# Decoder layer with sliding-window attention and retention: bursts of matmuls joined, a quad's vector work handed out in parts

## The chip, the cores and the metric

The kernel runs on one core of one Trainium2 chip. Measured is the device time of one execution in microseconds (us); smaller is better. The profile is of one execution on the same core.

## What is computed

One decoder layer on 256 tokens of width 2048: a SwiGLU feed-forward, a token-mixing part, a second feed-forward, each behind an RMS norm with scale and shift from a condition vector. The change touches the token mixing alone:

```python
rq, rk, rv, rg, sq, sk, sv, gl_ret, gl_swa = jnp.split(h @ w_in, IN_SPLITS, axis=-1)
# retention, 8 heads: q and k 128 wide (rotary), v 256 wide, two chunks of 128 tokens
ro = retention_chunkwise(rq, rk, rv)          # decayed scores @ v, no softmax
ro = ro * rsqrt(mean(ro * ro, -1) + eps)
# attention: 32 query heads, 8 key/value heads, 64 wide, window 128, one sink per head
logits = einsum('bnqhgd,bnkhd->bnhgqk', qb, kb) * d ** -0.5     # masked to the window
probs = softmax(concatenate([logits, sink], -1))[..., :-1]
out = einsum('bnhgqk,bnkhd->bnqhgd', probs, vb)
merged = sigmoid(gl_ret) * (ro' @ w_ret_branch) + sigmoid(gl_swa) * (out @ w_swa_branch)
```

All is float32 in and out.

## The kernel before

**The main work.** Every large product is a chain of weight blocks. `load` (L344 to L347) fetches a block of 512 rows by 512 columns, 1 MB, with a DMA that SyncE (SP) issues into one of four `raw` tiles. A block is used in two halves of 256 rows. For a half, `split` (L365 to L373) makes the pair `wh` and `wl`: ScalarE casts the half to the matmul's format (L369, `wh`), VectorE subtracts to get the rest (L371, `wl`). Pool `wsp` holds three such pairs. `products` (L349) then issues 12 matmuls of 512 columns for the half on TensorE: L356 and L357 read `wh`, L359 reads `wl`. `gemm_part` (L408) does one block: two halves, and a call of `tick` (L313) behind each. `gemm` calls `step` (L334) behind each block, which advances whatever generator stands first in the list `side`. So one block is one step of side work. The `raw` tiles are shared with the rows of `w_ada`, which a second stream (`conditioning`, L214 and L219) reads in the background.

**The side work.** While the blocks of `w_in` run, `softmax_heads` (L1321) does the attention: eight "quads" of four heads, four steps (parts 0 to 3) for a quad. For quad g:

- part 0, `quad_weights`: matmuls of queries and keys (L1229) into two banks of `psd` and two of `psm`; VectorE scales and masks them into `logits` (L1237), takes maxima (L1249 to L1253); ScalarE does the exponentials (L1258); VectorE adds and inverts the sums (L1262, L1263) and multiplies (L1265, two instructions).
- part 2, `quad_apart`: four ScalarE copies (L1279) split the words of the probabilities into the two planes of `planes_of`.
- part 2 of the next quad, `quad_turn`: two DMA transposes (L1288) issued by SP, from `planes_of` into tiles `a`. In that part `quad_turn` of the quad before comes ahead of `quad_apart` of this one.
- part 3 of the next quad, `quad_together`: four VectorE copies (L1300).
- part 1 two quads later, `quad_values`: matmuls of probabilities and values (L1313) and one copy (L1317).

`logits`, `planes_of` and `turned_p` exist once. After the quads come the eight heads of `retention` (L1395): step one makes the scores (L1398, L1401) and multiplies them by the decay; step two makes the values (L1411 to L1413), a root, and a scaling.

**What sets the order.** SP issues strictly in the order in which the program is written (L102). On the other engines a scheduler places instructions by priority and by its own estimate of when they are ready; `issue_after(x)` puts an instruction behind x on its engine. Every engine executes its instructions in the order in which they stand.

Of the kernel before, what the change touches and what calls it, by code (L numbers as in the profile page):

```python
# [17 lines left out]
P = 128  # L18
# [59 lines left out]
def layer_kernel(  # L78
# [57 lines left out]
    def a512():  # L136
        return t512()
# [1079 lines left out]
    halves = [slice(i * HD, (i + 1) * HD) for i in range(2)]  # L1217
    asked, dec = set(), []

    def quad_weights(g):  # L1220

        assert g // 2 in asked
        late = [side_bank() for _ in range(2)]
        early_q = [bank() for _ in range(2)]
        with tc.issue_after(newest[-1]), tc.high_priority(offset=300):
            for ps, qs, n in ((late, slice(P, S), S), (early_q, slice(0, P), P)):
                for a in range(2):
                    for i, hs in enumerate(halves):
                        nc.tensor.matmul(  # L1229
                            ps[i][:, a * n : (a + 1) * n],  # L1230
                            qo[hs, 2 * g + a, qs], skt[hs, g, :n], start=True, stop=True,
                        )
        by_half = logits.rearrange("p (a i) n -> p a i n", a=2)
        for ps, ns in ((late, slice(P, W3)), (early_q, slice(0, P))):
            n = ns.stop - ns.start
            for i in range(2):
                nc.vector.scalar_tensor_tensor(  # L1237
                    out=by_half[:, :, i, ns],
                    in0=ps[i][:, : 2 * n].rearrange("p (a n) -> p a n", a=2),
                    scalar=HD**-0.5,  # L1240
                    in1=mask[:, None, ns].broadcast_to([P, 2, n]),
                    op0=ALU.mult,
                    op1=ALU.add,
                )
        mx, ng, se, sm = (small(2 * HQ, tag) for tag in ("mx", "ng", "se", "sm"))
        m2, n2, s2 = (v.rearrange("p (t i) -> p t i", t=2) for v in (mx, ng, se))
        parts_of = (logits[:, :, :P], logits[:, :, P:])
        for t, of_t in enumerate(parts_of):
            nc.vector.tensor_reduce(out=m2[:, t, :], in_=of_t, axis=AX.X, op=ALU.max)  # L1249
        sb = sink_b[:, HQ * g : HQ * (g + 1)][:, None, :].broadcast_to([P, 2, HQ])  # L1250
        nc.vector.tensor_tensor(out=m2, in0=m2, in1=sb, op=ALU.max)
        nc.vector.tensor_scalar(out=ng, in0=mx, scalar1=-1.0, scalar2=None, op0=ALU.mult)
        nc.vector.tensor_tensor(out=s2, in0=n2, in1=sb, op=ALU.add)  # L1253
        nc.scalar.activation(se, se, AF.Exp)
        for t, of_t in enumerate(parts_of):
            for i in range(HQ):
                z = t * HQ + i
                nc.scalar.activation(  # L1258
                    of_t[:, i, :], of_t[:, i, :], AF.Exp,
                    bias=ng[:, z : z + 1], accum_out=sm[:, z : z + 1],  # L1260
                )
        nc.vector.tensor_add(sm, sm, se)  # L1262
        nc.vector.reciprocal(sm, sm)  # L1263
        for t, of_t in enumerate(parts_of):
            nc.vector.tensor_tensor(  # L1265
                out=of_t, in0=of_t,
                in1=sm[:, t * HQ : (t + 1) * HQ][:, :, None].broadcast_to(
                    [P, HQ, of_t.shape[2]]
                ),
                op=ALU.mult,  # L1270
            )

    def quad_apart():

        with tc.issue_after(cast[-1]):
            for a in range(2):
                src = logits[:, 2 * a : 2 * a + 2, :].rearrange("p h n -> p (h n)")
                for i in range(2):
                    nc.scalar.copy(planes[:, a, i, :], words(src)[:, :, i])  # L1279

    def quad_turn():

        turned = [pair_tile() for _ in range(2)]
        turned = [
            t.rearrange("p i n -> p (i n)").bitcast(U16)[:, : 4 * W3] for t in turned
        ]
        for a in range(2):
            nc.sync.dma_start_transpose(  # L1288
                turned[a].rearrange("p (k n) -> p k n", n=P),
                planes[:, a].rearrange("p i n -> p (i n)"),  # L1290
            )
        return turned

    def quad_together(turned):

        for a in range(2):
            into = turned_p[:, 2 * a : 2 * a + 2].rearrange("p h b q -> p (h b q)")
            with tc.issue_after(low[-1]):
                for i in range(2):
                    nc.vector.tensor_copy(  # L1300
                        words(into)[:, :, i], turned[a][:, i * 2 * W3 : (i + 1) * 2 * W3]
                    )

    def quad_values(g):

        po = bank()
        p4 = po.rearrange("p (a t q) -> p a t q", a=2, t=NT)
        vs = slice(g * HD, (g + 1) * HD)
        heads = turned_p.rearrange("p (a i) b q -> p a i b q", a=2)
        with tc.issue_after(newest[-1]), tc.high_priority(offset=300):  # L1310
            for t, blk, tv in ((0, 0, 0), (1, 1, 0), (1, 2, 1)):
                for i in (1, 0):
                    nc.tensor.matmul(  # L1313
                        p4[halves[i], :, t, :], sv[:, tv, vs], heads[:, :, i, blk, :],
                        start=blk < 2, stop=blk != 1,
                    )
        nc.any.tensor_copy(  # L1317
            qo[:, 2 * g : 2 * g + 2, :].rearrange("p a s -> p (a s)"), po
        )

    def softmax_heads():  # L1321

        turned = {}
        for at in range(4 * (QUADS + 1) + 2):
            g, part = divmod(at, 4)
            if part == 0 and g < QUADS:
                quad_weights(g)
            if part == 1 and g >= 2:
                quad_values(g - 2)
            if part == 2 and g >= 1:  # L1330
                turned[g - 1] = quad_turn()
            if part == 2 and g < QUADS:
                quad_apart()
            if part == 3 and g >= 1:
                quad_together(turned.pop(g - 1))
                if g == QUADS:
# [55 lines left out]

    vo = slot().rearrange("p (t n) -> p t n", t=NT)

    def retention(h):  # L1395
        assert {(0, h // 4), (1, h // 4)} <= kept
        ps = side_bank()
        nc.tensor.matmul(  # L1398
            ps[:, :S], qk[:, 1, h, :P], qk[:, 0, h, :], start=True, stop=True
        )  # L1400
        nc.tensor.matmul(  # L1401
            ps[:, S : S + P], qk[:, 1, h, P:], qk[:, 0, h, P:], start=True, stop=True
        )
        sc = a512()
        dh = dec[0][:, h * S : (h + 1) * S]
        nc.vector.tensor_mul(sc[:, :S], ps[:, :S], dh)
        nc.vector.tensor_mul(sc[:, S : S + P], ps[:, S : S + P], dh[:, :P])
        yield
        hv = slice(h * RDV, (h + 1) * RDV)
        po = side_bank()  # L1410
        nc.tensor.matmul(po[:, :RDV], sc[:, :P], vo[:, 0, hv], start=True, stop=True)  # L1411
        nc.tensor.matmul(po[:, RDV:], sc[:, P:S], vo[:, 0, hv], start=True, stop=False)  # L1412
        nc.tensor.matmul(  # L1413
            po[:, RDV:], sc[:, S : S + P], vo[:, 1, hv], start=False, stop=True
        )
        v = small(NT, "rvar")
        junk = a512()
        for t in range(NT):
            nc.scalar.activation(
                junk[:, t * RDV : (t + 1) * RDV],  # L1420
                po[:, t * RDV : (t + 1) * RDV],
                AF.Square,
                accum_out=v[:, t : t + 1],
            )
# [12 lines left out]
        yield  # L1437

    for ci in range(4):
        b = in_chunk(O_RV + ci * CH)  # L1440
        for t in range(NT):
            nc.any.tensor_copy(vo[:, t, ci * CH : (ci + 1) * CH], b[t])
        side += [retention(h) for h in (2 * ci, 2 * ci + 1)]

    def gates(p):

# [171 lines left out]
```

## Time and profile before

| | us |
|---|---|
| median of 3 runs (lowest, highest) | 2374.83 (2372.2, 2376.29) |
| the profiled execution, whole | 2372.74 |
| span of its instructions | 2370.9 |
| TensorE (PE) busy in it | 2343.8 (99%) |
| VectorE (DVE) busy | 1702.1 (72%) |
| ScalarE (ACT) busy | 1313.8 (55%) |
| first L1229 to last L1229 | 876.4 to 1052.7 |
| last L1313 | 1109.1 |

A row of a timeline holds the start, the duration, the engine, the line, the operation, the tiles written and read, a count, and in brackets how long the engine stood idle ahead of it and for whom. SPq is SyncE's queue of DMA issues, PEld the weight load of a matmul. A row of waits holds who waited for whom, the sum, how often, and the longest.

### The profile page before, as it was taken

The page shows a single profiled execution, that of the slowest core. Times are in us where ns is not written, and L with a number is a line of the kernel's source. Part 1 is how long each engine was busy: PE and PEld are TensorE (multiplying, and loading weights), DVE is VectorE, ACT ScalarE, POOL GpSimd, SP SyncE. Part 2 cuts the span into 40 slices and gives each one's busy share as a digit, 9 for nine tenths or more (in the row PEclk, how much of TensorE's full clock was granted, in tenths as well). Part 3 has the DMA queues.
Part 4 walks back from the last instruction along what each step waited for, and adds up shares of the span by engine and source line. Part 5 has one row for each costly group of instructions (what it writes and reads, how often), then busy time and mean ns, then how long its engine had stood idle before and what let it go on. Part 6 is the DMA issues. An engine that isn't in the chain of part 4 may idle for free.

```text
span 2370.9 us, 28253 instructions
## 1 busy us (share of the span) xinstructions
PE 2343.8 (99%) x10431; PEld 1917.6 (81%) x10431; DVE 1702.1 (72%) x2624; ACT 1313.8 (55%) x1782; POOL 9.2 (0%) x21
## 2 busy tenths in 40 slices
PE   8999999999999999999999999999999999999998
PEld 5888888888788887778888888888888888888886
DVE  7887799778877768976777776677555555555656
ACT  6544456455546568775556564466455455455544
POOL 0000000000000000000000000000000000000000
PEclk9999999999999999999999999999999999999999
DMA  9987789998866788877778787755677777766553
GB/s 367 366 294 264 272 292 343 356 351 336 312 248 241 274 281 235 252 223 244 270 274 294 297 299 281 289 197 185 240 240 250 253 241 247 245 220 203 192 198 124
DMA packets 186316, 627.87 MB, mean 265 GB/s; under 512 B 108801, under 2 KB 109185, under 8 KB 115649
## 3 DMA queue, kind: packets, MB, share of 16 engines
q1 hardware_dynamic: 183682, 615.05, 74.7%
q0 software_dynamic: 1600, 9.83, 1.2%
q8 instruction: 82, 1.34, 0.2%
q10 hardware_dynamic: 896, 1.19, 0.1%
q14 instruction: 56, 0.46, 0.1%
HBM read 597.16 MB, written 4.22 MB: 254 GB/s over the span
## 4 chain that ended last, share of the span: by engine, by line
PE 54%; DVE 1%; DMA 0%; issue 0%; ACT 0%; DVEq 0%; SPq 0%
PE pa L359 18%; PE pa L356 18%; PE pa L357 18%; DMA slot<-in_w_ada_dram 0%; DVE wl L371 0%; PE ps L1313 0%; PE pd L1411 0%; PE pd L1413 0%; PE pd L1412 0%; PE pd L1398 0%; PE ps L832 0%; DVE home L465 0%; ACT wh L369 0%; DVE soft L1300 0%; DVE slot L219 0%
## 5 line engine op out<-in xcount | busy, mean ns | idle before, releaser
L369 ACT CAST wh<-raw 128x1024 fp32r<-128x1024 f32 x792 | 832.0, 1053 | 913.2 <-PE pa L357 888.6
L371 DVE TENSOR_TENSOR wl<-raw,wh 128x1024 fp32r<-128x1024 f32 x792 | 961.1, 1222 | 520.3 <-ACT wh L369 518.5
L356 PE MATMUL pa<-wh,hh 128*128 128x512 f32 x2184 | 854.1, 391 | 2.4 <-ACT wh L369 2.4
L357 PE MATMUL pa<-wh,hl 128*128 128x512 f32 x2184 | 850.4, 389 | 0.0
L359 PE MATMUL pa<-wl,hh 128*128 128x512 f32 x2184 | 773.6, 391 | 2.6 <-DVE wl L371 2.4
L356 PEld LDWEIGHTS pa<-wh,hh 128*128 128x128 f32 x2184 | 410.0, 188 | 91.0 <-ACT wh L369 3.7
L359 PEld LDWEIGHTS pa<-wl,hh 128*128 128x128 f32 x2184 | 408.4, 188 | 92.8 <-DVE wl L371 7.0
L357 PEld LDWEIGHTS pa<-wh,hl 128*128 128x128 f32 x2184 | 410.1, 188 | 84.6 <-issue 0.2
L357 PE MATMUL pa<-wh,a 128*128 128x512 f32 x944 | 366.2, 389 | 0.0
L356 PE MATMUL pa<-wh,a 128*128 128x512 f32 x944 | 349.9, 390 | 1.8 <-DVE t L622 1.8
L359 PE MATMUL pa<-wl,a 128*128 128x512 f32 x944 | 348.4, 390 | 1.9 <-DVE wl L371 1.9
L219 DVE CUSTOM_DVE_ANT_0 slot<-slot,cact 128x512 f32<-128x512 f32 (+2 forms) x272 | 209.7, 819 | 22.5 <-DMA slot<-in_w_ada_dram 22.4
L359 PEld LDWEIGHTS pa<-wl,a 128*128 128x128 f32 x944 | 177.0, 188 | 39.8 <-DVE wl L371 3.4
L356 PEld LDWEIGHTS pa<-wh,a 128*128 128x128 f32 x944 | 177.0, 188 | 39.2 <-DVE t L622 2.2
L357 PEld LDWEIGHTS pa<-wh,a 128*128 128x128 f32 x944 | 177.3, 188 | 37.9 <-DVE a L405 1.3
L530 ACT COPY slot<-back 128x512 uint16<-128x512 uint16 x140 | 93.3, 766 | 0.0
L219 DVE CUSTOM_DVE_ANT_0 rows_x<-rows_x,cact 128x512 f32<-128x512 f32 x124 | 78.7, 686 | 13.3 <-DMA rows_x<-in_w_ada_dram 13.1
L219 DVE CUSTOM_DVE_ANT_0 raw<-raw,cact 128x512 f32<-128x512 f32 (+1 forms) x108 | 70.8, 706 | 16.1 <-DMA raw<-in_w_ada_dram 16.1
L405 DVE TENSOR_TENSOR a<-slot,a 128x512 fp32r<-128x512 f32 x118 | 80.5, 684 | 0.3
L514 ACT COPY flat<-t 128x512 uint16<-128x512 uint16 x128 | 72.7, 617 | 3.6 <-DVE t L1386 2.8
L404 ACT CAST a<-slot 128x512 fp32r<-128x512 f32 x118 | 72.7, 617 | 0.1
L219 DVE DVE_READ_ACCUMULATOR2_ANT sums<- 128x1 f32 x504 | 41.0, 81 | 0.0
(228 smaller groups left out, 1169.1 us busy)
## 6 DMA issues: line engine op xcount, KB each, us to landing
raw<-in_w_ffn_gu_dram SPq DMA_DIRECT2D x160, 1024.0 KB, 5.1
raw<-in_w_in_dram SPq DMA_DIRECT2D x104, 1024.0 KB, 5.7
raw<-in_w_ffn_down_dram SPq DMA_DIRECT2D x88, 1024.0 KB, 4.9
slot<-in_w_ada_dram SPq DMA_DIRECT2D x83, 1024.0 KB, 7.2
rows_x<-in_w_ada_dram SPq DMA_DIRECT2D x31, 1024.0 KB, 7.1
raw<-in_w_ada_dram SPq DMA_DIRECT2D x26, 1024.0 KB, 5.6
raw<-in_w_swa_branch_dram SPq DMA_DIRECT2D x16, 1024.0 KB, 6.8
raw<-in_w_ret_branch_dram SPq DMA_DIRECT2D x16, 1024.0 KB, 5.6
```

What stands on the lines that cost most here:

```text
L219: nc.vector.tensor_tensor_reduce(out=w[:, at], in0=w[:, at], in1=cact[:, at], scale=1.0, scalar=0.0, op0=ALU.mult, op1=ALU.add, accum_out= ...
L356: nc.tensor.matmul(ps, ah[:, j, ts], wh[:, j, :], start=first, stop=False)
L357: nc.tensor.matmul(ps, al[:, j, ts], wh[:, j, :], start=False, stop=False)
L359: nc.tensor.matmul(ps, ah[:, j, ts], wl[:, j, :], start=False, stop=last).ins
L369: cast.append(nc.scalar.copy(hi, src).ins)
L371: low.append(nc.vector.tensor_sub(lo, src, hi.bitcast(F32)).ins)
L404: nc.scalar.copy(hi, v)
L405: nc.vector.tensor_sub(lo, v, hi.bitcast(F32))
L514: nc.scalar.copy(planes[:, i, :], words(src)[:, :, i])
L530: nc.scalar.copy(into[:, :, :, i], held["turned"][:, i])
```

## The change

For the quads, the class `Quad` takes the place of `quad_weights`, `quad_apart`, `quad_turn` and `quad_together`. The matmuls of the values of quad g-2 and of the logits of quad g are issued by one call, `quad_burst`, in part 0, and share the two banks of `psm`; the values' copy is two ScalarE copies in part 2. The vector work is put into a list `trickle`, from which `tick` takes one entry behind each half of a block. The sink is negated once, which lets two VectorE instructions of a quad fall away. For retention, `head_burst` issues the values of head h-2 with the scores of head h, a step for a head, 11 steps in place of 16.

```diff
+    trickle = []
+
     def tick():
+        if trickle:
+            trickle.pop(0)()
...
+    def quad_burst(g, gv):
...
+        late = [side_bank() for _ in range(2)] if g is not None else None
+        both = [bank() for _ in range(2)]
         with tc.issue_after(newest[-1]), tc.high_priority(offset=300):
+            if gv is not None:
...
+                            both[t][halves[i], S:].rearrange("p (a q) -> p a q", a=2),
+                            sv[:, tv, vs], heads[:, :, i, blk, :],
...
+            if g is not None:
+                assert g // 2 in asked
+                for ps, qs, n in ((late, slice(P, S), S), (both, slice(0, P), P)):
...
             g, part = divmod(at, 4)
-            if part == 0 and g < QUADS:
-                quad_weights(g)
-            if part == 1 and g >= 2:
-                quad_values(g - 2)
-            if part == 2 and g >= 1:
-                turned[g - 1] = quad_turn()
-            if part == 2 and g < QUADS:
-                quad_apart()
-            if part == 3 and g >= 1:
-                quad_together(turned.pop(g - 1))
...
+            now, past = quads.get(g), quads.get(g - 1)
+            assert not trickle
+            if part == 0:
+                late, both = quad_burst(
+                    g if g < QUADS else None, g - 2 if g >= 2 else None
+                )
...
+                if past:
+                    trickle.extend([lambda: past.apart(0), lambda: past.apart(1)])
+            if part == 1:
+                if past:
+                    past.turn()
+                if now:
+                    trickle.extend([now.masked, now.greatest])
...
+            if part == 2 and g >= 2:
+                quad_out(g - 2, both)
+            if part == 2 and now:
+                trickle.extend([lambda: None, lambda: now.powers(0)])
+            if part == 3:
+                def parts(i):
+                    if now and i == 0:
+                        now.powers(1)
+                    if past:
+                        past.together(i)
+                    if now and i == 1:
+                        now.shares()
+
+                trickle.extend([lambda: parts(0), lambda: parts(1)])
```

`apart` is the four ScalarE copies (now L1329), `turn` the two transposes (now L1338), `shares` the sum, reciprocal and multiplications (now L1313 to L1316), each with the instructions that it had, but for two small VectorE ones.

SP, at the transposes of the second quad (g = 1), before. `raw` blocks count up in the order of their numbers; `a` are the tiles that the transposes of a quad write, `back` those of other transposes:

```order
L346 DMA raw_7208<-in_w_in_dram 128x2048
L346 DMA raw_7288<-in_w_in_dram 128x2048
L519 DMA_TRANSPOSE back_7322<-flat_7027 128x8x128
L346 DMA raw_7335<-in_w_in_dram 128x2048
L519 DMA_TRANSPOSE back_7370<-flat_7104 128x8x128
L1288 DMA_TRANSPOSE a_7372<-planes_of 128x12x128
L1288 DMA_TRANSPOSE a_7373<-planes_of 128x12x128
L346 DMA raw_7380<-in_w_in_dram 128x2048
```

ScalarE, before, at the copies that fill `planes_of` for these transposes:

```order
L369 CAST wh_7210<-raw_7208 128x1024
L1279 COPY planes_of<-soft 128x768 x4
L369 CAST wh_7227<-raw_7208 128x1024
L530 COPY slot_6287<-back_7102 128x4x128 x2
L530 COPY slot_6287<-back_7144 128x4x128 x2
L369 CAST wh_7290<-raw_7288 128x1024
L369 CAST wh_7306<-raw_7288 128x1024
L514 COPY flat_7247<-t_7192 128x512 x2
L369 CAST wh_7337<-raw_7335 128x1024
L514 COPY flat_7324<-t_7199 128x512 x2
L369 CAST wh_7354<-raw_7335 128x1024
L369 CAST wh_7382<-raw_7380 128x1024
```

So before, behind the copies ScalarE has five casts (7227, 7290, 7306, 7337, 7354) of blocks that SP issued ahead of the transposes. Over the eight quads that number is 5, 5, 5, 4, 5, 2, 5, 6. The same place on SP after the change:

```order
L350 DMA raw_7191<-in_w_in_dram 128x2048
L350 DMA raw_7263<-in_w_in_dram 128x2048
L523 DMA_TRANSPOSE back_7301<-flat_7023 128x8x128
L1338 DMA_TRANSPOSE a_7306<-planes_of 128x12x128
L1338 DMA_TRANSPOSE a_7307<-planes_of 128x12x128
L350 DMA raw_7310<-in_w_in_dram 128x2048
```

And ScalarE after the change:

```order
L373 CAST wh_7265<-raw_7263 128x1024
L373 CAST wh_7283<-raw_7263 128x1024
L518 COPY flat_7242<-t_7175 128x512 x2
L518 COPY flat_7303<-t_7182 128x512 x2
L1329 COPY planes_of<-soft 128x768 x4
L373 CAST wh_7312<-raw_7310 128x1024
L373 CAST wh_7333<-raw_7310 128x1024
```

Now the last block issued ahead of the transposes, raw_7263, is cast ahead of the copies, and the next cast is of raw_7310, which SP issues behind the transposes: the number is 0, for this quad and for all eight. VectorE after the change, at the same place (L1316 are the multiplications that the copies read):

```order
L375 TENSOR_TENSOR wl_7266<-raw_7263,wh_7265 128x1024
L375 TENSOR_TENSOR wl_7284<-raw_7263,wh_7283 128x1024
L1314 RECIPROCAL sm_7129<-sm_7129 128x8
L1316 TENSOR_TENSOR soft<-soft,sm_7129 128x4x128
L1316 TENSOR_TENSOR soft<-soft,sm_7129 128x4x256
L375 TENSOR_TENSOR wl_7313<-raw_7310,wh_7312 128x1024
```

The multiplications stand behind the low part of raw_7263 and directly ahead of that of raw_7310; so they do for the quads 1 to 4 and the last, and two low parts earlier for the quads 0, 5 and 6.

TensorE after the change, at the first call that issues values and logits together (values of quad 0, logits of quad 2); before, the eight matmuls L1229 stood together, and the six of L1313 stood 32 main matmuls behind them:

```order
L1244 MATMUL pd_7245<-slot_6125,slot_6287 128x256
L1244 MATMUL pd_7246<-slot_6125,slot_6287 128x256
L360 MATMUL pa_7189<-wh_7265,hh_4025 128x512
L361 MATMUL pa_7189<-wh_7265,hl_4026 128x512
L360 MATMUL pa_7190<-wh_7265,hh_4025 128x512
L361 MATMUL pa_7190<-wh_7265,hl_4026 128x512
L1234 MATMUL ps_7247<-soft,slot_6125 64x256 x2
L1234 MATMUL ps_7248<-soft,slot_6125 64x256 x4
L1244 MATMUL ps_7247<-slot_6125,slot_6287 128x128
L1244 MATMUL ps_7248<-slot_6125,slot_6287 128x128
```

Half of the logits stay a burst of their own, 1 or 4 main matmuls ahead of the values, in quads 2 to 5; in quads 6 and 7 all stands together. Counting all eight quads there are 14 bursts in place of 16. In retention there are 10 in place of 18.

More of the change, by code (lines that the diff above doesn't have):

```diff
@@ L1294, in quad_together, with turn, together @@
-    def quad_together(turned):
-        for a in range(2):
+        def turn(self):
+            self.turned = [
+                pair_tile().rearrange("p i n -> p (i n)").bitcast(U16)[:, : 4 * W3]
+                for _ in range(2)
+            ]
+            for a in range(2):
+                nc.sync.dma_start_transpose(
+                    self.turned[a].rearrange("p (k n) -> p k n", n=P),
+                    planes[:, a].rearrange("p i n -> p (i n)"),
+                )
+        def together(self, a):
@@ L1297, in quad_together @@
             into = turned_p[:, 2 * a : 2 * a + 2].rearrange("p h b q -> p (h b q)")
-            with tc.issue_after(low[-1]):
+            with tc.issue_after(low[-1]), tc.high_priority(offset=300):
                 for i in range(2):
                     nc.vector.tensor_copy(
-                        words(into)[:, :, i], turned[a][:, i * 2 * W3 : (i + 1) * 2 * W3]
-                    )
[L1304 to L1319, printed above, removed]
@@ new lines, in together @@
+                        self.turned[a][:, i * 2 * W3 : (i + 1) * 2 * W3],
+                    )
+    def softmax_heads():
+        quads = {}
+        with tc.issue_after(low[-1]):
+            nc.vector.tensor_scalar(
+                out=sink_b, in0=sink_b, scalar1=-1.0, scalar2=None, op0=ALU.mult
+            )
+        for at in range(4 * (QUADS + 1) + 3):
+            g, part = divmod(at, 4)
+            now, past = quads.get(g), quads.get(g - 1)
[3 more added lines that the diff above has]
+                    g if g < QUADS else None, g - 2 if g >= 2 else None
+                )
+                if late:
+                    quads[g] = Quad(g, late, both)
+                if past:
[5 more added lines that the diff above has]
+                    trickle.extend([now.masked, now.greatest])
+                elif g == QUADS:
@@ L1436, in retention, with retention_heads @@
             )
-        yield
+    def retention_heads():
+        for h in range(RH + 3):
+            while h // 2 not in valued and h < RH:
+                yield
+            if 1 <= h <= RH:
+                head_masked(h - 1)
+            if h >= 3:
+                head_scaled(h - 3)
+            if h < RH + 2:
+                head_burst(h)
+            yield
+    side.append(retention_heads())
     for ci in range(4):
```

207 lines of the change are left out of this document (114 added, 93 removed).

## The prediction

> **What bounds the kernel now.** First the page's own lines: one engine fills the span.
>
> ```profile
> span 2370.9 us, 28253 instructions
> PE 2343.8 (99%) x10431; PEld 1917.6 (81%) x10431; DVE 1702.1 (72%) x2624; ACT 1313.8 (55%) x1782; POOL 9.2 (0%) x21
> ```
>
> PE is busy 2343.8 of 2370.9 us, so at most 27 us of waiting can be won anywhere. Then the list of waits over the whole span:
>
> ```profile
> ACT wh L369 <- PE pa L357: 888.6, 599, 3.3
> DVE wl L371 <- ACT wh L369: 518.5, 432, 4.2
> ```
>
> ACT mostly waits for PE to give a `wh` tile back: the makers of weights run ahead of PE as far as three tiles allow. Next PE's timeline in the stage that is changed, first burst of logits; start, then duration, are the columns to read.
>
> ```profile
> 876.08 0.39 PE L359 MATMUL pa<-wl,hh 128*128 128x512 f32 x1
> 876.40 1.13 PE L1229 MATMUL pd<-slot,slot 64*128 64x256 f32 x8
> 877.37 0.61 PE L1229 MATMUL ps<-slot,slot 64*128 64x128 f32 x8
> 877.91 0.50 PE L356 MATMUL pa<-wh,hh 128*128 128x512 f32 x1
> 878.25 0.39 PE L357 MATMUL pa<-wh,hl 128*128 128x512 f32 x1
> ...
> 878.71 0.39 PE L356 MATMUL pa<-wh,hh 128*128 128x512 f32 x1
> ...
> 881.44 0.39 PE L356 MATMUL pa<-wh,hh 128*128 128x512 f32 x1
> ```
>
> From 878.71 to 881.44 stand 12 main matmuls, one half of a block: 2.73 us, 0.227 us each. That is PE's pace when nothing is missing. Entering the burst takes 0.32 (876.08 to 876.40), leaving it 0.34 (877.91 to 878.25): 0.09 and 0.11 over the pace, so a pair of borders costs 0.20 us. The burst itself fills 1.51. And the stage of the quads, seven of the eight, by engine (span; PE, PEld, DVE, ACT and POOL busy):
>
> ```profile
> 876.00:1051.00 175.00, 173.55 (x846) 138.01 (x845) 143.60 (x242) 136.03 (x264) 0.00 (x0) 1.00 0.83 230
> ```
>
> PE loses 1.45 of 175 us here; a quad takes 25.0 us, of which DVE works 143.60 / 7 = 20.5. There is little to win, and DVE has 4.5 us a quad to spare.
>
> **The change, part by part.**
>
> **Joined bursts.** By the order of the changed program the quads keep 14 bursts of 16: 2 x 0.20 = 0.4 us less. The switch from 64-row to 128-row matmuls inside a joined burst is in no row; between nothing and a whole pair of borders, eight times, it is 0 to 1.6. In retention 10 bursts take the place of 18, at most 8 x 0.20 = 1.6 saved, and nothing if these borders are free; here is one such pair, already together by chance:
>
> ```profile
> 1195.90 0.39 PE L359 MATMUL pa<-wl,hh 128*128 128x512 f32 x1
> 1196.13 0.59 PE L1411 MATMUL pd<-slot,t 128*128 128x256 f32 x2
> ...
> 1197.99 0.48 PE L356 MATMUL pa<-wh,hh 128*128 128x512 f32 x1
> ```
>
> It is entered after 0.23, the plain pace, so little is left to join there. Bounds of the part: -2.0 to +1.6; I take 0.
>
> **Fewer and smaller vector pieces.** Two DVE instructions of some 0.17 us a quad fall away. They lie on DVE, which is not what ends PE's waits here, and all but 1.45 us of PE is already filled: between -1.5 (all of that wait gone) and 0; I take 0.
>
> **The transposes on SP.** This is the part that I expect to decide. SP is one queue, and the two transposes of a quad wait in it for ACT's copies into `planes_of`; the block loads written behind them wait too. SP's waits between 850 and 1210 us:
>
> ```profile
> SPq L346 <- DVE wl L371: 99.6, 26, 7.9
> SPq L1288 <- ACT planes_of L1279: 22.6, 4, 11.8
> ```
>
> The first row says that SP normally issues a load as soon as DVE frees a `raw` tile, so SP comes to the transposes early; the second that it then stands there, up to 11.8 us. Before, that is harmless because 4 to 6 halves of blocks already fetched lie behind the copies on ACT. In one quad, the sixth, there are 2. SP's and ACT's timeline there:
>
> ```profile
> 1025.03 3.35 SPq L1288 DMA_TRANSPOSE a<-planes_of  x2
> 1028.44 4.35 SPq L346 DMA_DIRECT2D raw<-in_w_in_dram  x4
> ```
>
> ```profile
> 1023.43 3.04 ACT L1279 COPY planes_of<-soft 128x768 uint16<-128x768 uint16 x4
> 1026.36 1.06 ACT L369 CAST wh<-raw 128x1024 fp32r<-128x1024 f32 x1
> 1029.22 1.05 ACT L369 CAST wh<-raw 128x1024 fp32r<-128x1024 f32 x1 [1.80 <-PE pa L357]
> 1035.32 1.05 ACT L369 CAST wh<-raw 128x1024 fp32r<-128x1024 f32 x1 [5.04 <-DMA raw<-in_w_in_dram]
> ```
>
> And DVE and PE:
>
> ```profile
> 1036.40 1.23 DVE L371 TENSOR_TENSOR wl<-raw,wh 128x1024 fp32r<-128x1024 f32 x1 [3.48 <-ACT wh L369]
> ...
> 1040.22 0.20 DVE L1263 RECIPROCAL sm<-sm 128x8 f32<-128x8 f32 x1
> 1040.46 1.83 DVE L1265 TENSOR_TENSOR soft<-soft,sm 128x512 f32<-128x512 f32 x2
> ```
>
> ```profile
> 1046.59 0.73 PE L359 MATMUL pa<-wl,hh 128*128 128x512 f32 x2 [0.97 <-DVE wl L371]
> ```
>
> The chain reads: copies start 1023.43; transposes issue from 1025.03 (1.60 later); they hold SP until the load at 1028.44 (3.41); its block is there and cast at 1035.32 (6.88); its low part starts at 1036.40 (1.08). Together 12.97 us, of which ACT had two casts' worth of cover, and stood idle 5.04. PE lost 0.97 ten microseconds later, its only wait for weights of any size in the stage beside one of 0.48.
>
> The change puts `apart` and `turn` one step apart. By the order of the changed program all eight quads have 0 halves behind the copies, where 4 to 6, once 2, stood. The block behind each pair of transposes is asked for only when ACT and DVE have nothing left to make.
>
> Price by cover: the sixth quad lost 0.97 with two halves in hand; without them PE has 2 x 2.73 = 5.45 us less to work on, so it loses 0.97 + 5.45 = 6.4 us a quad, 8 x 6.4 = **51 us**.
>
> Price by DVE's round: in the quads 1 to 4 and 7 the multiplications stand right ahead of the waiting low part, so DVE idles the whole 13.0 us; it then has 20.5 of work before it comes round: 33.5 a quad for 25.0. Over seven rounds 7 x 8.5 = 60. Quads 0, 5 and 6 keep two low parts behind the multiplications, 2 x 1.23 each, which brings it to 60 - 7 = 53.
>
> Lower bound: PE with all it can hold at the last cast, three halves and a joined burst (3 x 2.73 + 1.51 + 1.44 = 11.1, the last from the rows below), against 12.97 until the next cast is done (1023.43 to 1036.37), plus the low part, reciprocal and multiplications (1.23 + 0.20 + 1.83) ahead of the copies: 16.2 - 11.1 = 5.1 in the five quads where they stand there, 12.9 - 11.1 = 1.8 in three: 31 us. With the load's median landing of 5.9 in place of the 6.88, 1 us less each: 23.
>
> ```profile
> 933.15 1.52 PE L1313 MATMUL ps<-soft,slot 128*64 128x256 f32 x12
> 934.59 0.50 PE L359 MATMUL pa<-wl,hh 128*128 128x512 f32 x1
> ...
> raw<-in_w_in_dram SPq DMA_DIRECT2D x59, 1024.0 KB, 5.9
> ```
>
> I take 51: it rests on a loss that a row of this stage shows, and the round of DVE comes to nearly the same. Nothing moves SP's other queue neighbours for the worse beyond this: a row of `w_ada` is asked for once in 16 halves (a quarter of one of its four passes behind each half). POOL has only the load of the decay, which comes after the quads.
>
> **Sum.** 0 + 0 + 51 on the profiled execution's 2372.7: 2424 us (+2.1%). The median of the runs is 2.1 above that execution, within their spread; the forecast stays 2424.
>
> **The rivals.**
>
> *The cover holds better.* ACT and DVE enter each quad with all that PE can hold. For it: the 888.6 us that ACT waits for PE. Against it: at 1046.59 PE ran dry 10 us after the late block had come, since what ACT and DVE make ahead is not soon made up, and DVE is busy 82% of the stage. Time: 2372.7 + 23 to 31, about 2400.
>
> *PE loses its clock as well.* PE would stand several microseconds eight times. The start of the span shows what follows a long wait: the same four matmuls, first and second time.
>
> ```profile
> 17.28 3.78 PE L1008 MATMUL pa<-raw,t 128*128 128x512 f32 x4 [1.76 <-ACT t L607]
> ...
> 23.58 1.98 PE L1008 MATMUL pa<-raw,t 128*128 128x512 f32 x4 [0.23 <-ACT t L607]
> ```
>
> 3.78 for 1.98: 1.8 us more, while the waits of up to 1.8 us in the middle of the span are followed by the plain pace. With 1.8 behind each of eight waits and the round of DVE at its upper 60: 2372.7 + 60 + 14 = 2447. Against it: what PE loses while DVE is the later one costs nothing. The Trainium skill has this rule (TensorE: Matmul & The Clock Gate, "What's actually happening"): an idle window of about 3.4 us halves the PE clock until PE has been busy for as long. The granted clock of the stage before, 1.00, agrees in so far as no wait there is that long; no run yet shows the rule at work in mid-span.
>
> *Not slower.* If ACT's copies come earlier than SP reaches the transposes, SP never stands, and what is left is the gain: the waits of 0.97 and 0.48 gone and 0.4 of borders, 2372.7 - 1.9 = 2371. It decides at the cast of the last block ahead of the transposes: SP would have to be less than one block ahead of ACT. Against it: SP waits 99.6 us for `raw` tiles, that is, it is as far ahead as four tiles allow. For it: if the loads come late for another reason.
>
> That the bursts are not joined as the change says is true for quads 2 to 5 and already in the sum.
>
> **How the numbers follow.** Forecast 0.60; cover holds 0.20; clock 0.13; not slower 0.07. The range leaves out the not-slower case, and the outer edges of the next two: 2372.7 + 21 to + 80, 2394 to 2453, about 0.82 in it. A measurement of this kernel tells from no change about 0.2%, 4.7 us. Slower by more than that in the first three: 0.92, with 0.01 lost to the cover's lowest edge; the not-slower case is within 0.2% (-1.9 us), 0.06 with that edge, and 0.02 faster if more waits than named go.
>
> **What would show it.** Right: SP waits for `planes_of` in all eight quads, some 10 us each; ACT's casts wait for the DMA of `raw` some 5 to 8 us a quad; DVE idles about 13 us behind the multiplications; PE waits for `wh` or `wl` some 6 us a quad, and first to last logits burst grows from 176 to near 220 us, with everything after 1210 only shifted. The joined bursts show at 3.2 to 3.4 us for six of L1234 and the logits. Wrong: SP's wait without a wait on PE (cover), PE's main matmuls at twice 0.227 behind each wait (clock), or no wait for `planes_of` on SP at all; also a stall in retention, where I expect none.

## The result and the profile after

The changed kernel takes 2449.99 us, median of 4 runs (2447.47 to 2450.62), against 2374.98 before (2372.2 to 2376.29): ratio 1.0315, 95% interval 1.0303 to 1.0327. That is 75 us slower; forecast were 2424 us in a range of 2394 to 2453. The direction and the place were right. The forecast is 26 us low.

The page of the changed kernel, first the span and the engines (busy us, share, instructions):

```profile
span 2448.8 us, 28243 instructions
PE 2364.0 (97%) x10431; PEld 1924.4 (79%) x10431; DVE 1701.3 (69%) x2616; ACT 1313.3 (54%) x1789; POOL 9.2 (0%) x21
```

DVE and ACT work as long as before (1702.1 and 1313.8 us). The span has grown by 77.9 us. PE counts 20 us more as busy, and the rest is idle. The waits over the whole span (sum, times, longest):

```profile
DVE wl L375 <- ACT wh L373: 623.1, 458, 12.3
...
ACT wh L373 <- DMA raw<-in_w_in_dram: 78.9, 18, 8.7
...
PE pa L360 <- ACT wh L373: 52.5, 12, 7.7
```

Three rows read as one chain: ACT waits for a block's DMA, up to 8.7 us at a time, DVE for ACT, PE for ACT. Set the same numbered main matmul of both traces side by side, and the lag is 0.65 us ahead of the quads, 73.7 behind them, and 77.9 at the end. So 73 us are lost in the stage, 4 behind it. Now one quad of it. ACT, from the copies on:

```profile
1044.32 3.04 ACT L1329 COPY planes_of<-soft 128x768 uint16<-128x768 uint16 x4 [0.64 <-issue]
1055.04 1.99 ACT L373 CAST wh<-raw 128x1024 fp32r<-128x1024 f32 x2 [7.69 <-DMA raw<-in_w_in_dram]
```

No cast stands between the copies and the wait: the "0 halves in hand" of the order. SP's queue at that time:

```profile
1045.91 3.30 SPq L1338 DMA_TRANSPOSE a<-planes_of  x2
1049.26 0.87 SPq L350 DMA_DIRECT2D raw<-in_w_in_dram  x1
```

The chain is the predicted one: copies to transposes 1.59 (predicted 1.60), the pair to the load 3.35 (3.41), load to cast 5.78 (6.88). PE, behind the wait that this makes:

```profile
1048.75 0.39 PE L363 MATMUL pa<-wl,hh 128*128 128x512 f32 x1
1056.14 0.79 PE L360 MATMUL pa<-wh,hh 128*128 128x512 f32 x1 [7.00 <-ACT wh L373]
1056.73 0.63 PE L361 MATMUL pa<-wh,hl 128*128 128x512 f32 x1
1057.15 0.63 PE L360 MATMUL pa<-wh,hh 128*128 128x512 f32 x1
1057.58 0.63 PE L361 MATMUL pa<-wh,hl 128*128 128x512 f32 x1
1058.01 1.05 PE L363 MATMUL pa<-wl,hh 128*128 128x512 f32 x2
1058.86 0.63 PE L360 MATMUL pa<-wh,hh 128*128 128x512 f32 x1
1059.29 0.49 PE L361 MATMUL pa<-wh,hl 128*128 128x512 f32 x1
1059.62 0.40 PE L363 MATMUL pa<-wl,hh 128*128 128x512 f32 x1
```

The starts are 0.43 us apart until 1059.29 and 0.23 after it: PE has lost half its clock. All eight long waits look like this. Added up over the stage: eight waits of 3.8 to 7.7 us, 49.9 us together; 62 matmuls at 0.43 in place of 0.227, 62 x 0.203 = 12.6 us; smaller waits, 4.8. Together that is 67 of the 73 us.

That says where PE's time went, not what set the pace. A round through DVE does, from one quad's copies to the next:

```profile
1042.38 1.85 DVE L1316 TENSOR_TENSOR soft<-soft,sm 128x512 f32<-128x512 f32 x2
1056.12 1.22 DVE L375 TENSOR_TENSOR wl<-raw,wh 128x1024 fp32r<-128x1024 f32 x1 [11.88 <-ACT wh L373]
1057.26 1.28 DVE L1274 SCALAR_TENSOR_TENSOR soft<-pd,small_c 128x512 f32<-128x512 f32 x2
...
1074.56 1.83 DVE L1316 TENSOR_TENSOR soft<-soft,sm 128x512 f32<-128x512 f32 x2
```

DVE stands 11.88 us behind the multiplications, then works through a whole quad with pauses of 2.46 and 0.38 us, and with the next multiplications the copies and the next standing begin. Over the seven rounds from the first quad's copies to the eighth's (span; PE, PEld, DVE, ACT, POOL busy; clock), before and after:

```profile
890.32:1064.80 174.48, 173.36 (x849) 137.48 (x850) 144.86 (x245) 134.47 (x262) 0.00 (x0) 1.00 0.85 241
```

```profile
901.00:1142.56 241.56, 194.17 (x877) 147.48 (x876) 145.54 (x241) 134.91 (x266) 0.00 (x0) 0.92 0.57 174
```

DVE's work is the same, 144.86 and 145.54 us, 20.7 and 20.8 a round. Its idle time is 4.2 us a round before and 13.7 after. A round has gone from 24.9 to 34.5 us on average. One by one the seven are 37.5, 34.4, 36.8, 34.7, 32.5, 31.1 and 34.6 us. The standing behind the multiplications takes 11.0 to 12.3 us of each (8.6 and 2.7 in the first round); the rest of the idle time is pauses of up to 2.5 us, in which DVE waits for ACT's `wh` or, in the first and third round, for PE's sum `pa` (L1429).

### The profile page after: what moved, and what is told of

It reads as the page before. It is cut to its first block, busy times and chain, and to the rows that moved or that the text cites. A ratio compares the mean times of both kernels' runs of the same rounds, so it can differ in the third digit from the quotient of the medians.

```text
span 2448.8 us, 28243 instructions
## 1 busy us (share of the span) xinstructions
PE 2364.0 (97%) x10431; PEld 1924.4 (79%) x10431; DVE 1701.3 (69%) x2616; ACT 1313.3 (54%) x1789; POOL 9.2 (0%) x21
## 4 chain that ended last, share of the span: by engine, by line
PE 50%; DVE 2%; DMA 2%; ACT 1%; issue 1%; SPq 0%; DVEq 0%; ACTq 0%
PE pa L363 17%; PE pa L360 16%; PE pa L361 16%; DMA raw<-in_w_in_dram 1%; DVE wl L375 1%; DMA rows_x<-in_w_ada_dram 1%; ACT wh L373 0%; SPq L1338 0%; DMA slot<-in_w_ada_dram 0%; DVE rows_x L219 0%; ACT planes_of L1329 0%; PE ps L1462 0%; PE pd L1468 0%; PE ps L1459 0%; PE ps L1458 0%
```

## The experiments

Two theories were put against each other at first. Theory 1: the transposes stand one step behind the copies, SP's queue stands at them, and the block behind them comes late. Theory 2: the vector work in small parts, or the joined bursts, cost the time. Eleven runs followed; ratios are against before on the same chip, with 95% intervals.

| run | us | ratio |
|---|---|---|
| transposes one block later | 2398.16 | 1.0094 (1.0074 to 1.0113) |
| transposes two blocks later | 2380.76 | 1.0020 (1.0011 to 1.0030) |
| before, transposes early | 2453.37 | 1.0330 (1.0311 to 1.0350) |
| 24 narrow matmuls ahead of each wait | 2465.47 | 1.0378 (1.0358 to 1.0398) |
| their tile alone | 2462.61 | 1.0364 (1.0350 to 1.0379) |
| 24 wide matmuls ahead of each wait | 2465.45 | 1.0379 (1.0363 to 1.0395) |
| before with the new retention | 2375.93 | 0.9998 (0.9989 to 1.0006) |
| two blocks later, old retention | 2382.05 | 1.0022 (1.0013 to 1.0031) |
| changed, masking twice | 2462.14 | 1.0364 (1.0348 to 1.0379) |
| two blocks later, masking twice | 2383.97 | 1.0038 (1.0025 to 1.0050) |
| two blocks later, pace of rows as before | 2375.72 | 1.0001 (0.9992 to 1.0010) |

**Transposes one block later.**

```diff
-            if part == 1:
-                if past:
-                    past.turn()
+            if part == 2 and past:
+                past.turn()
+            if part == 1:
                 if now:
```

> The changed kernel with one thing moved: the two transposes of a quad stand one block later in the program (part 2 in place of part 1), so SP asks for one more block ahead of them. By the order of the program 1, 1, 0, 1, 1, 2, 2, 2 already fetched halves then lie behind the copies on ScalarE, in place of 0 in all eight quads. Theory 1 (SP's queue: the block behind the transposes is asked for too late, and TensorE runs at a lower clock behind each long wait): ten halves at 2.73 us are 27 us of the 50 us of waits, and most of the 13 us of the clock goes with them, as waits fall under 4 us: 2400 to 2425 us, SP's wait on planes_of shorter than 84.8 us. Theory 2 (the vector work put into the trickle, or the joined bursts, cost the time): nothing they contain is altered, so the time stays within 5 us of 2450.

Measured 2398.16, so 52 us of the 75 are gone with one line moved and the trickle and bursts untouched. PE's long waits fell from eight of 49.9 us to four of 10.9 (1.70, 1.77, 4.42, 3.03). That is 39 us, not the 27 that I got from the ten halves counted in the order: the block moved is worth nearly its full 5.45 us of matmuls in each quad. The time came out 2 us below the range given. SP's row for `planes_of`, expected below 84.8 us, is 91.0 here, but that row alone misleads: SP's whole standing did shrink, as the next run shows.

**Transposes two blocks later** (the same, with part 3).

> The changed kernel with the two transposes of a quad two blocks later (part 3): by the order of the program 3, 3, 2, 3, 3, 3, 3, 4 fetched halves lie behind the copies. Theory 1: three halves are 8.2 us, more than the 6.2 us that a quad waited, so the waits and the low clock go: 2370 to 2378 us, no wait of TensorE over 2 us in the stage, the joined bursts and the trickle as they are. Theory 2: still within 5 us of 2450. Between the two (2380 to 2440) would say that a part of the loss is the trickle's.

Measured 2380.76: 69 of the 75 us gone, 3 us over the range expected. ACT at one quad:

```profile
1010.01 3.04 ACT L1329 COPY planes_of<-soft 128x768 uint16<-128x768 uint16 x4 [1.36 <-DVE soft L1316]
1012.95 2.00 ACT L373 CAST wh<-raw 128x1024 fp32r<-128x1024 f32 x2
1014.85 0.64 ACT L1254 COPY slot<-ps 128x256 f32<-128x256 f32 x2
1015.58 1.05 ACT L373 CAST wh<-raw 128x1024 fp32r<-128x1024 f32 x1
1020.70 1.05 ACT L373 CAST wh<-raw 128x1024 fp32r<-128x1024 f32 x1 [4.06 <-DMA raw<-in_w_in_dram]
```

Three casts of blocks in hand stand between the copies and the wait, and the wait is 4.06 in place of 7.69 us, too short to reach PE. SP's waits for `planes_of`, in this kernel and then in the changed one (850 to 1290 us), the second with its other large rows of the same line:

```profile
SPq L1338 <- ACT planes_of L1329: 93.1, 8, 14.8
```

```profile
SPq L1338 <- ACT planes_of L1329: 84.8, 7, 15.3
SPq L1338 <- DVE se L1294: 40.7, 5, 14.0
SPq L1338 <- ACT wh L373: 23.5, 1, 23.5
SPq L1338 <- DVE soft L1348: 18.6, 2, 9.4
```

One standing is put down to several releasers, so the `planes_of` rows can't be set against each other. SP's timeline gives the whole of it, from the end of the issue ahead to the first transpose of each quad: 16.1 to 23.3 us in the changed kernel, 163 in all; 104 in all with the transposes one block later; 6.7 to 13.4 us, 87 in all, here; 37 in all in the kernel before. So SP stands less than in the changed kernel, but more than twice as long as before, and that costs almost nothing. The wait of a queue is not the loss; what is fetched already when it begins decides. Theory 2 is down to the last 5 us.

**The kernel before, with nothing but the transposes moved.**

```diff
-            if part == 2 and g >= 1:
-                turned[g - 1] = quad_turn()
+            if part == 3 and g < QUADS:
+                turned[g] = quad_turn()
```

> The kernel before, with nothing of the change but the place of the transposes: in part 3 of the same quad in place of part 2 of the next. Bursts apart, vector work in one piece. By the order of the program 0 fetched halves lie behind the copies in all eight quads. Theory 1: the loss of the change appears without it, 50 us of waits and some 13 us of low clock, somewhat more or less as the vector work stands otherwise: 2425 to 2455 us. Theory 2: within 5 us of 2375.

Measured 2453.37: the whole loss, without joined bursts and without the trickle. Set at the same main matmuls, its stage lost 74.6 us, the changed kernel's 73.

```profile
PE pa L356 <- ACT wh L369: 56.9, 10, 10.5
ACT wh L369 <- DMA raw<-in_w_in_dram: 54.0, 9, 9.1
```

The same two rows carry it as in the changed kernel. With the run before, this settles the cause in both directions.

**Work put into the waits.** The next three runs ask whether PE's 12.6 us of slow matmuls are a loss of their own.

```diff
+                if pad[0] and t == halves[-1] and j == n - 1:
+                    pad[0] -= 1
+                    for _ in range(0 if pad[0] else 24):
+                        nc.tensor.matmul(
+                            ps[:16, :], blank[0], ah.rearrange("p k s -> p (k s)"),
+                            start=False, stop=False,
+                        )
...
+        blank.append(one.tile([P, 16], F32R, tag="blank", name="blank"))
+        nc.vector.memset(blank[0].bitcast(F32), 0.0)
...
                     trickle.extend([lambda: past.apart(0), lambda: past.apart(1)])
+                    pad[0] = 2
```

> The changed kernel with 24 more matmuls of 512 columns (a block of zeros, 16 columns wide, times hh, added to the running sum) ahead of the last matmul before each of the eight long waits: 24 x 0.227 = 5.45 us of work put into waits of 3.8 to 7.7 us, which overfills three of them by 2.9 us in all. The disputed point is the 13 us of matmuls at 0.43 us instead of 0.227 behind each wait. If they come from TensorE having stood too long (clock), the waits left are under 2.3 us, the slow matmuls go, and the time falls to 2437 to 2443 us although there is more work. If they come from late weights, or the pace has another reason, nothing is won: 2449 to 2455 us, with the slow matmuls still behind the waits.

Measured 2465.47, above both expectations. The matmuls of this kernel lie 0.229 us apart in much of the span, and not 0.227, from the start of the program on, so it can't be held against the changed kernel. The tile without the matmuls (`range(0)`) is the right partner:

> The changed kernel with the small block of zeros alone (16 columns a partition, from the last free memory) and none of the additional matmuls. In the run with 24 of them TensorE's common pitch was 0.229 us in place of 0.227 over the whole execution, from the first matmuls on, long before the first additional one. If the tile, which shifts other tiles in memory, does that, the time is 2460 to 2470 us here too, at 0.229. If the additional matmuls do it, or it was that job, the time is within 4 us of 2450, at 0.227.

Measured 2462.61, at 0.229: the tile does it. Between the two, seven rounds of copies; first the tile alone, then with the matmuls:

```profile
908.20:1152.26 244.06, 197.43 (x877) 149.63 (x876) 145.56 (x241) 135.26 (x265) 0.00 (x0) 0.90 0.57 173
```

```profile
908.88:1152.95 244.07, 228.02 (x1032) 158.17 (x1032) 144.42 (x241) 134.60 (x266) 0.00 (x0) 0.97 0.57 173
```

168 of the 192 additional matmuls fall into the seven rounds, 168 x 0.229 = 38 us of work; the granted clock is up from 0.90 to 0.97, the slow matmuls in the stage are down from 76 to 30 (15 to 6 us at 0.2 each), and the seven rounds are 244.06 and 244.07 us. Here is what the work fills:

```profile
951.98 5.72 PE L365 MATMUL pa<-hh,blank 128*16 128x512 f32 x24
957.53 0.39 PE L370 MATMUL pa<-wl,hh 128*128 128x512 f32 x1
960.14 0.50 PE L360 MATMUL pa<-wh,hh 128*128 128x512 f32 x1 [2.21 <-ACT wh L380]
```

PE's wait, its slow matmuls, and 5.55 us of work that nobody needs take each other's place, and the rounds hardly move: PE's time is not what they add up. That the sums agree to 0.01 us is luck. The single rounds moved by +1.2, +0.7, +0.2, -0.1, +0.4, -0.4 and -1.9 us; the last one has its multiplications one low part earlier. Set at the same main matmuls, the stage is 1.9 us shorter with the additional work, where 9 us of slow matmuls went; the three overfilled waits may hide up to 2.9 us more. So most of the slow matmuls' time was no loss of its own; a smaller part may have been. The 2.9 us between the two whole times lie within the spread of the runs.

The wide form (`hh` as weights, `blank` repeated over 512 columns):

> As the run with 24 additional matmuls ahead of each long wait, but 128 columns wide (hh as the weights, the zeros repeated over 512 columns), so that each uses all of the array. If the 30 matmuls at 0.43 us that were left there came from narrow matmuls counting as little work, they go here, and the stage is 6 us shorter than there: first to last logits burst 240 us or less. If they came from the waits alone (1.7 to 2.2 us that were left), about as many stay. Either way theory 1 says that the waits shrink by what is put in and the time is no shorter than the changed kernel's by more than 13 us: 2437 to 2453 us at a pitch of 0.227, 15 us more at 0.229.

Measured 2465.45, and again 30 slow matmuls: the width of the additional matmuls is not what left them.

**Retention alone, and the old retention.**

```diff
-    def retention(h):
+    valued, scores, sums_of, values = set(), {}, {}, {}
+    def head_burst(h):
...
-        side += [retention(h) for h in (2 * ci, 2 * ci + 1)]
+        valued.add(ci)
```

> The kernel before with the changed kernel's retention (bursts of values and scores joined, 10 bursts in place of 18, eleven steps in place of sixteen) and nothing else of the change. The prediction's step on joined bursts: between -1.6 and +1.6 us, I take 0, so 2373 to 2377 us. A rival, from the trace of the run with the transposes two blocks later: its stage of quads cost 0.2 us against before, but about 2 us came ahead of it and 2 to 4 us of small waits for wl and wh behind the retention (main matmuls 5200 to 6400). If the retention makes these, the time is 2 to 4 us above that of before, and the waits show there.

> The counterpart: the changed kernel's quads with the transposes in part 3, and the retention of before. If the retention makes the small waits behind it, this is within 2 us of before (2373 to 2377 us), 3 to 5 us faster than with both (2380.8); if the quads' own new order makes them, it stays at 2379 to 2382 us. The joined bursts of the quads and the trickle are all in it, so their cost is what is left above before.

Measured 2375.93 and 2382.05. Joining the bursts of the retention is worth nothing within 0.1%, and the last 5 us of the kernel with late transposes do not come from it. My rival here was wrong; the quads make them.

**More work for DVE.**

```diff
-                for ps, ns in ((self.late, slice(P, W3)), (self.early_q, slice(0, P))):
+                for ps, ns in 2 * ((self.late, slice(P, W3)), (self.early_q, slice(0, P))):
```

> The changed kernel with each quad's masking of the logits written twice (four more VectorE instructions a quad, the same values again): (10.3 + 6.0) / 8 = 2.04 us more VectorE work a quad, and nothing else. It tells apart what sets the changed kernel's pace in the stage. If it is VectorE's round (12.9 us of standing behind the copies, then its 20 us of work, then the next quad's multiplications and copies; TensorE only waits inside it), each quad is 2.04 us longer: 8 x 2.04 = 16 us, 2462 to 2470 us. If it is TensorE (its waits and its slow matmuls one after the other, as the sum by cover has it), VectorE's 61% of the stage leaves room and the time stays at 2448 to 2454 us.

> The same doubled masking in the kernel with the transposes in part 3, as the control: there VectorE does not stand behind the transposes and has some 4 us a quad to spare, so by the round 2.04 us more a quad cost nothing: 2379 to 2386 us (two quads have 1 and 2 fetched halves behind the copies here in place of 3, which could cost a wait of some microseconds). If VectorE's work costs its own length wherever it stands, 2397 us.

Measured 2462.14, some 12 us more than the changed kernel, and 2383.97 for the control, 3 us more than without. The seven rounds with the masking twice:

```profile
900.05:1153.51 253.46, 197.03 (x884) 151.96 (x884) 160.58 (x273) 133.21 (x261) 0.00 (x0) 0.89 0.54 166
```

DVE's work is up by 160.58 - 145.54 = 15.0 us, the rounds by 253.46 - 241.56 = 11.9. In the sum DVE pays for four fifths of what it is given, where PE had 38 us added at next to no cost. Round by round it is less clean: the first four grew by 0.2, 0.8, 0.5 and 0.2 us, the last three by 4.8, 3.4 and 2.0, for some 2.1 us of work each. In the first four the work went into pauses: behind the long standing DVE has gaps of 1.4 to 1.8 us there in the changed kernel, and none over 0.3 in this one. In the last three the edit did more than add work: the scheduler put the multiplications of quads 5 and 6 directly ahead of the waiting low part, where the changed kernel has two low parts behind them. So the run shows that DVE's work counts once its pauses are full. That DVE's work alone sets every round it does not show, and how much of the last three rounds' 10.2 us is the new order stays open.

**The pace of the rows.** What was left were 5 us, of which some 3 stand behind the stage as small waits for `wl` and `wh`.

```diff
+            if at == 4 * (QUADS + 1) + 2:
+                pace["rate"] = RATE_AFTER
+                turns.append(rows_beside())
             yield
-        pace["rate"] = RATE_AFTER
-        turns.append(rows_beside())
```

> The kernel with the transposes in part 3, and the faster pace of the background sums (rows of w_ada) set one block earlier, at the block at which the kernel before sets it: the changed quads take one step more than the old ones. It asks about the 4 us of small waits for wl and wh (main matmuls 5200 to 6400) that stand behind the stage with either retention, and not with the retention alone. If that one step is the reason, by which VectorE's passes over w_ada stand otherwise against the weights, the time is 2375 to 2378 us; if something else in the quads' order is, it stays at 2379 to 2383 us.

Measured 2375.72, ratio 1.0001 (0.9992 to 1.0010), and from the end of the quads to 1600 us no wait of PE is left. The changed quads have 39 steps where the old ones have 38, so the rows of `w_ada` came one block later against the weights. With both places mended, joined bursts and vector work in parts together are worth nothing: no version tried here beats the kernel before.

## Why the prediction was right or wrong

**Joined bursts, 0 (bounds -2.0 to +1.6): right.** A joined burst of the changed kernel:

```profile
1075.59 0.39 PE L363 MATMUL pa<-wl,hh 128*128 128x512 f32 x1
1075.91 1.14 PE L1244 MATMUL pd<-slot,slot 64*128 64x256 f32 x8
1076.97 1.52 PE L1234 MATMUL ps<-soft,slot 128*64 128x256 f32 x12
1078.42 0.72 PE L1244 MATMUL ps<-slot,slot 64*128 64x128 f32 x8
1079.06 0.50 PE L360 MATMUL pa<-wh,hh 128*128 128x512 f32 x1
1079.40 0.39 PE L361 MATMUL pa<-wh,hl 128*128 128x512 f32 x1
```

From 1075.59 to 1079.40 less two paces of 0.227 it costs 3.36 us, as said (3.2 to 3.4), and as much as logits (1.71) and values (1.65) apart: the scheduler put the values between two groups of logits, and the switch costs what the border saved. Where the values stand first, in the kernel with late transposes, it is 3.16, a border of 0.2 saved. Eight times that is 1.6 us at most, below what a measurement tells.

**Fewer vector pieces, 0: right.** One small instruction a quad falls away, not two: three (L1251 to L1253) became two (L1291, L1294), and DVE's count goes from 2624 to 2616. DVE's busy time is within 1 us, and the mended version equals before.

**The transposes on SP, +51: the right mechanism, mis-sized; the stage lost 73.** SP stood at them in every quad, for 16 to 23 us where some 10 were predicted, and the links of the chain behind it are about as long as predicted. What failed is the step "8 x 6.4 = 51", the price by cover. It priced PE's waits, and those it hit (49.9). But it took PE's missing supply for the whole loss, while the added work in the waits shows that PE's time was not what the stage adds up; what PE waits for, and how slowly it then runs, follows mostly from a round that has its length elsewhere. The other price, by DVE's round, was the better one. It said 13.0 of standing and 20.5 of work, 33.5 a round; measured are 20.8 of work and 13.7 idle, 34.5. But the standing is only 11.0 to 12.3 of that, and the pauses, which the price left out, make up for it: that the round came so near is in part luck. Its sum came out too low in two ways. Over the seven rounds it said 53, and they grew by 241.56 - 174.48 = 67: the rounds without low parts behind the multiplications of the next quad take 35.6 on average, not 33.5. The two that lead to quads 5 and 6, with such low parts, are the shortest (32.5 and 31.1), so the relief that it took off may be there; no run separates it. And it counted seven rounds for eight quads: the first standing, with its 4.75 us wait, and the last one's follow-up, together 73 - 67 = 6 us, were left out. Eight times 34.5 - 24.9 = 9.6 would have been 77 us, for a measured 73.

**"PE waits some 6 us a quad":** 6.2 on average. **First to last logits burst "near 220":** 233.2 (877.8 to 1111.0).

**The rivals.** *The cover holds* (2400) is out. *PE loses its clock* happened, with 12.6 us by PE's own account, close to the 14 named, and its total of 2447 is near the result; but that is luck for the most part, for the two prices don't add. The argument set against it, that what PE loses while DVE is the later one costs nothing, held in the main: with the slow matmuls reduced from 15 to 6 us, the stage became 1.9 us shorter. The Trainium skill's rule (TensorE: Matmul & The Clock Gate, "What's actually happening") that an idle window of some 3.4 us halves the clock is now shown in mid-span, by the rows at 0.43 above. That less than a whole window of idling is enough, the last section shows. *Not slower* is out: SP was far ahead, as the 99.6 us spoke for.

**Retention, "no stall":** right for the retention. Missed were the 4 us behind it, from a step more in the quads: I had looked at what the additional steps moved on SP and not at the pace that the end of the quads sets for DVE.

## What to carry to other kernels

Before work is put between a producer and a transfer that waits for it on an in-order queue, count how many fetched blocks stand behind the producer on the engine that will run dry: here one block of distance was worth 52 us, two 69, and the length of the queue's own wait said little: 87 us of standing cost almost nothing. When a stall recurs in a cycle, follow the cycle through one whole turn (the transfer, the work that waits for it, the pauses in that work), and price the stall there, for every turn; waits and slow clocks of engines beside it fill the same gap and must not be added. To find what sets the length, put a known amount of useless work on each candidate, read each turn and not only the sum, and see in the trace that the order stayed as it was.

## What was not expected of the hardware

**The slow clock comes in fixed windows.** In the changed kernel the last slow matmuls of the eight groups end at 916.0, 953.4, 987.6, 1025.0, 1059.3, 1093.3, 1124.3 and 1158.1 us. The distances, 37.4, 34.2, 37.4, 34.3, 34.0, 31.0 and 33.8, are 11, 10, 11, 10, 10, 9 and 10 times 3.41 within 0.3 us, less than one slow matmul; the ends of the waits miss such multiples by up to 0.8. In the run with 24 narrow matmuls the four groups end at 933.9, 964.6, 1009.1 and 1074.0, 9, 13 and 19 times 3.41 apart. The granted clock agrees. Here are four windows of that length around the wait shown above, which ended at 1056.14 (span; PE, PEld, DVE, ACT, POOL busy; clock):

```profile
1049.26:1052.67 3.41, 0.00 (x0) 0.00 (x0) 0.00 (x0) 0.00 (x0) 0.00 (x0) 1.00 1.06 242
1052.67:1056.08 3.41, 0.00 (x0) 0.00 (x0) 0.00 (x0) 1.04 (x2) 0.00 (x0) 0.50 1.01 394
1056.08:1059.49 3.41, 3.35 (x8) 2.68 (x9) 3.37 (x6) 1.54 (x4) 0.00 (x0) 0.50 1.10 346
1059.49:1062.90 3.41, 3.41 (x16) 2.78 (x16) 3.41 (x10) 1.82 (x3) 0.00 (x0) 1.00 1.01 423
```

After an idle window the next one has half the clock, and after a busy one the next has all of it. A wait need not fill a window. In the run with the transposes one block later this was enough:

```profile
944.89 0.39 PE L363 MATMUL pa<-wl,hh 128*128 128x512 f32 x1
947.04 0.50 PE L360 MATMUL pa<-wh,hh 128*128 128x512 f32 x1 [1.77 <-ACT wh L373]
947.38 0.39 PE L361 MATMUL pa<-wh,hl 128*128 128x512 f32 x1
...
948.30 0.76 PE L363 MATMUL pa<-wl,hh 128*128 128x512 f32 x2
948.87 0.62 PE L360 MATMUL pa<-wh,hh 128*128 128x512 f32 x1
949.29 0.63 PE L361 MATMUL pa<-wh,hl 128*128 128x512 f32 x1
```

A wait of 1.77 us, then 1.8 us of matmuls at full pace, and only then slow ones, until 952.3. A wait of 1.70 earlier in the same run, which the grid cuts into 0.6 and 1.1, was followed by none. Laid on the grid of 3.41 us, the windows of the changed kernel and of the runs with late transposes and with added work agree: up to 1.5 us idle in a window at full clock, none slow after it; from 1.9 us, always; between 1.6 and 1.8, either. So half a window of idling is about the limit here, and the prediction's "waits of up to 1.8 us in the middle of the span are followed by the plain pace" held only by where those waits lay.

**A tile of 64 bytes a partition cost some 12 us.** It stands ahead of the pools from which the matmuls read, and with it alone the common distance of matmuls of 512 columns is 0.229 in place of 0.227 us in much of the span (2462.61 against 2449.99). That it is the addresses of the operands is likely and was not tried by itself.
